# A fourth buffer for the cast and low part of the attention probabilities, in space that the tile of split q and k does not use

## The chip, the cores and the metric

The kernel runs on one core of a Trainium2 chip. The metric is the device time of one execution in microseconds (us). The engines are named as in the profile: PE (TensorE: matmuls; PEld is its weight load), DVE (VectorE), ACT (ScalarE), POOL (GpSimd) and SP (SyncE, which issues nearly all DMAs here). Each engine works through its own instructions in a fixed order; an instruction that waits for a semaphore holds up all that stand behind it on the same engine.

## The reference

One layer of a transformer with two kinds of attention heads, on 2048 positions of width 1024, in float32:

```
u   = rms_norm(x, norm1_w);  p = u @ w_in          # 3072 columns: q, k, v of both kinds
# differential heads (4): two softmax maps a head
logits = q.k * scale + t5_bias, masked by chunks of 64
attn   = softmax(map 0) - lam * softmax(map 1);  y = attn @ v
# stick-breaking heads (8)
z      = q.k * scale
log_1mb = log_sigmoid(-z) for s < t, else 0
rem    = reverse_cumsum(log_1mb) - log_1mb
a      = exp(log_sigmoid(z) + rem) for s < t, else 0;  y = a @ v
# both: rms_norm of y a head, then
h = x + concat(y_diff, y_sb) @ w_out
out = h + (silu(u2 @ w_gate) * (u2 @ w_up)) @ w_down,   u2 = rms_norm(h, norm2_w)
```

## The kernel before

PE multiplies in float16. To keep float32's accuracy every operand is split in two: `hi`, the value cast to float16, and `lo`, the cast of what is left. A product is then three matmuls, hi*hi, hi*lo and lo*hi.

**Head groups.** `block` takes the heads in eight groups, `g` 0 to 3 for one differential head each and 4 to 7 for two stick-breaking heads each. For a group, `proj` computes 384 columns of `p` (q, k and v) for 16 tiles of 128 positions: a tile of normed, transposed `x` is read back from DRAM as `xt` (line 395, three buffers), and 24 matmuls (line 329) go to `pj`. `proj_out` splits v into `v`, and q and k into `st` (lines 348 to 354). Each four tiles `proj_batch` transposes `st` by DMA into `qT` and `kT` (line 381). In the differential groups it first norms q and k, with `st` also as scratch for their squares (line 363). The projection of the next group is issued in between the attention of the present one (`advance`).

**Units of attention.** A unit is a block of 128 queries against up to 1024 keys. The differential `probs` makes z by scores, maximum, `Exp` and the subtraction of the two maps (line 516). The stick-breaking `stage_a` has for every 512 keys: scores on PE (`sc`), two sigmoids on ACT (lines 563, 566), a running product on DVE (line 568) and a product on DVE or POOL (line 569). Either way the probabilities of a unit then go through `split_t`:

```
s16 = s16p.tile([P, 2048], F16, tag="s16", bufs=SB, name=nm("s16"))
to16(s16[:, :n], src, n, he)
tt(s16[:, n : 2 * n], src, s16[:, :n], ALU.subtract, n, le)
aT = sp.tile([P, 16, P], F16, tag="aT", bufs=AB, name=nm("aT"))
SP.dma_start_transpose(aT[:, : 2 * n // P, :], s16[:, : 2 * n])
```

The cast (line 89 on ACT, line 93 on POOL) and the low part (line 98, on POOL) fill one `s16`, SP issues one transposing DMA from it into `aT` (line 412), and `pv` multiplies `aT` by v on PE (line 467). In the profile `s16` is called `s`. A buffer of `s16` is free again when its transpose has landed. There are `SB` = 3 of them and `AB` = 5 of `aT`; the stick-breaking part runs `pv` of a unit `PD` = 5 units after its `stage_a`.

**Output projection and feed-forward.** During the last group `out_proj` multiplies the finished rows by `w_out` and adds `x`, which it loads into `xf`, a tile with the tag of `st` (line 763) or spare space. `post` norms the rows and makes the seven combinations of blocks for the feed-forward part; they are split in tiles with the tag of `s16` as well (line 797, `x` in the profile) and stored to `xcd`. The feed-forward part follows, with its own pools over the space of the attention's pools.

**What sets the order.** The tile framework orders each engine's instructions when the program is built, with priorities and a simulated timeline (line 1238), and allots the buffers as it goes: an instruction that fills a tile has to come after the last use of that buffer's earlier tile. Which engine makes a cast or a subtraction is decided earlier, by the running cost sums of `pick` (lines 76 to 98), which do not know of buffers.

**Space.** The pool `s16p` (`bias` and the `s16` tiles) is on the left side of SBUF with `sp` and `zp`; `pp`, which holds `st`, is on the right side.

Of the kernel before, what the change touches and what calls it, by code (L numbers as in the profile page):

```python
# [11 lines left out]
F32 = mybir.dt.float32  # L12
F16 = mybir.dt.float16
# [8 lines left out]
S, D, P = 2048, 1024, 128  # L22
# [13 lines left out]
KW = {"A": 1.0, "D": 1.0, "P": 1.0}  # L36
AHEAD = 2
AHN = 0
QB, KB, ZB, AB, SB, PD = 4, 7, 9, 5, 3, 5
XL = (0, 4, 5, 2, 1, 6, 3)  # L40
CU = 3
WE = "AP"
# [17 lines left out]
def block(tc, a, out):  # L60
# [3 lines left out]
    with top:  # L64
# [8 lines left out]
        def note(e, ns):  # L73
            load[e] += ns * KW[e]
# [34 lines left out]
        def nm(s):  # L109
            uid[0] += 1  # L110
            return f"{s}{uid[0]}"
# [146 lines left out]
        pp = pjs.enter_context(tc.tile_pool(name="pp", bufs=2, side="right"))  # L258

        with ExitStack() as ph1:  # L260
# [61 lines left out]
            @pri("pm")  # L322
            def proj_tile(G, xt):
                pj = psj.tile([P, 512], F32, tag="pj", name=nm("pj"))
                xv = xt[:].rearrange("p (s k n) -> p s k n", s=2, k=KT)
                n = 0
                for kt in range(KT):
                    for xi, wi in ((0, 0), (0, 1), (1, 0)):
                        PE.matmul(pj[:, :384], lhsT=xv[:, xi, kt, :], rhs=G["w"][:, wi, kt, :], start=n == 0, stop=n == 23)  # L329
                        n += 1  # L330
                return pj
# [10 lines left out]
            @pri("po")  # L342
            def proj_out(g, G, pj, B, j):
                st, v, raw = B
                nv = 1 if g < 4 else 2
                vv = v[:, j, :].rearrange("p (h s e) -> p h s e", h=nv, s=2)
                split_psum(vv[:, :, 0, :], vv[:, :, 1, :], pj[:, 256:384].rearrange("p (h e) -> p h e", h=nv), 128)
                if g < 4:
                    if pick(A=270, D=335) == "A":
                        ACT.mul(raw[:, j, :], pj[:, :256], 2.0 ** -11)  # L350
                    else:
                        DVE.tensor_scalar(raw[:, j, :], pj[:, :256], 2.0 ** -11, None, op0=ALU.mult)
                else:
                    split_psum(st[:, 0:4, j, 0, :], st[:, 0:4, j, 1, :], pj[:, :256].rearrange("p (c e) -> p c e", c=4), 256)
# [33 lines left out]
            def proj(g, G, fresh=None):  # L388
                for t in range(NT):
                    if fresh is not None:  # L390
                        feed(t)
                        xt = ahead.pop(0)
                    else:
                        xt = pp.tile([P, 2 * D], F16, tag="xt", bufs=3, name=nm("xt"))
                        SP.dma_start(xt[:], xs[t])
                    if t % 4 == 0:
                        st = pp.tile([P, 6, 4, 2, 64], F16, tag="st", name=nm("st"))
                        v = sp.tile([P, 4, 256], F16, tag="v", bufs=KB, name=nm("v"))
                        raw = pp.tile([P, 4, 256], F32, tag="raw", name=nm("raw")) if g < 4 else None
                    pj = proj_tile(G, xt)  # L400
                    proj_out(g, G, pj, (st, v, raw), t % 4)
                    if t % 4 == 3:
                        proj_batch(g, G, (st, v, raw))
                    yield
# [223 lines left out]
            def feed(t):  # L628
                while nx[0] < min(NT, t + AHEAD + AHN):
                    nq.append(fresh(nx[0]))  # L630
                    nx[0] += 1
                while nx[1] < min(NT, t + AHEAD):
                    ahead.append(fresh_t(*nq.pop(0)))
                    nx[1] += 1
# [68 lines left out]
            def proj_stream():  # L703
                for g in range(NG):
                    for t, _ in enumerate(proj(g, Gs[g], fresh if g == 0 else None)):
                        if g == 0 and t == 0:
                            build_bias()
                        if g == NG - 1 and t in WT:
                            if t == WT[0]:
                                rp2.extend(norm_gain(a["norm2_w"], w2))  # L710
                            load_wo(WT.index(t))
                        if t == PF and g + 1 < NG:
                            Gs[g + 1] = load_w(g + 1)
                        yield
# [40 lines left out]
            def out_proj():  # L755
                for t in range(NT):
                    mt = pp.tile([P, 2 * D], F16, tag="xt", bufs=3, name=nm("mt"))[:].rearrange("p (k n) -> p k n", k=KT)
                    with tc.high_priority(PRI["wm"]) if PRI["wm"] else nullcontext():
                        mts.append(SP.dma_start(mt, ms[t]))
                    if t in spare:  # L760
                        xf = spare[t].bitcast(F32)
                    else:
                        xf = pp.tile([P, 6, 4, 2, 64], F16, tag="st", name=nm("xf"))[:].rearrange("p c t s e -> p (c t s e)").bitcast(F32)[:, :D]
                    SP.dma_start(xf, x[t * P : (t + 1) * P, :])
                    for h in range(2):
                        po = psj.tile([P, 512], F32, tag="pj", name=nm("po"))
                        for n in range(2):
                            q = 0
                            sl = slice(256 * n, 256 * n + 256)
                            for kt in range(KT):  # L770
                                for xi, wi in ((0, 0), (0, 1), (1, 0)):
                                    PE.matmul(po[:, sl], lhsT=mt[:, kt, P * xi : P * xi + P], rhs=wos[2 * h + n][wi][:, kt, :], start=q == 0, stop=q == 23)  # L772
                                    q += 1
                            xl = xf[:, 512 * h + 256 * n : 512 * h + 256 * n + 256]
                            DVE.scalar_tensor_tensor(xl, po[:, sl], kos[2 * h + n][:], xl, op0=ALU.mult, op1=ALU.add)  # L775
                    note("D", 1400)
                    SP.dma_start(hd[t], xf)
                    if t >= 12:
                        yield
                        continue  # L780
                    post(t, xf)
                    yield
# [3 lines left out]
            @pri("ox")  # L786
            def post(t, xf):
                if t % 2 == 0:
                    held[:] = [z4(), z4()]
                xn = held[t % 2]  # L790
                norm_tile(xf, xn[:, :D], w2)
                for h in range(2):
                    ACT.copy(xn[:, 512 * h : 512 * h + 512], transposed(xn, 512 * h)[:])
                note("D", 1150)
                note("A", 1000)
                if t % 2 == 1:
                    for _ in x_ops([z[:, :D].rearrange("p (d n) -> p d n", d=2) for z in held], z4()[:, :D].rearrange("p (d n) -> p d n", d=2), t // 8, t % 8 // 2, lambda: s16p.tile([P, 2048], F16, tag="s16", bufs=SB, name=nm("x16"))[:]):
                        pass

            op = out_proj()  # L800
            outs = 0
            advance(NT - LAG0)
# [439 lines left out]
```

## Time and profile before

| | |
|---|---|
| median of 3 runs | 2723.46 us (2717.96 to 2725.68) |
| the profiled execution | 2726.11 us |
| its span, first to last instruction | 2724.3 us |
| mean granted TensorE clock | 0.975 |

A wait in the profile is written `engine tile line <- what ended it: us in total, times, longest`. In a row of a table of stretches, each engine has its busy us and its count of instructions; after them stand the granted clock, the busy share of the 16 DMA engines and GB/s. A share over 1 is possible, since packets overlap in an engine. SP only issues, and has no busy time in these tables.

### The profile page before, as it was taken

The page shows a single profiled execution, that of the slowest core. Times are in us where ns is not written, and L with a number is a line of the kernel's source. Part 1 is how long each engine was busy: PE and PEld are TensorE (multiplying, and loading weights), DVE is VectorE, ACT ScalarE, POOL GpSimd, SP SyncE. Part 2 cuts the span into 40 slices and gives each one's busy share as a digit, 9 for nine tenths or more (in the row PEclk, how much of TensorE's full clock was granted, in tenths as well). Part 3 has the DMA queues.
Part 4 walks back from the last instruction along what each step waited for, and adds up shares of the span by engine and source line. Part 5 has one row for each costly group of instructions (what it writes and reads, how often), then busy time and mean ns, then how long its engine had stood idle before and what let it go on. Part 6 is the DMA issues. An engine that isn't in the chain of part 4 may idle for free. (4 is left out here: it accounts for less than half of the span.)

```text
span 2724.3 us, 45559 instructions
## 1 busy us (share of the span) xinstructions
PE 2471.4 (91%) x17084; PEld 1404.6 (52%) x17084; DVE 1945.7 (71%) x3716; ACT 1345.8 (49%) x2483; POOL 1569.3 (58%) x1134
## 2 busy tenths in 40 slices
PE   7998989898888786779888999999999999999998
PEld 4655655555555453557775444444444444444443
DVE  6898979698888988876666877777786544444445
ACT  4665656567878878765644535444352112111121
POOL 2577767667767777765655666575674232323223
PEclk9999999999999997999999999999999999999999
DMA  6788797779999998996797675666749744545534
GB/s 223 205 168 176 149 195 161 177 170 206 208 207 203 205 183 159 205 202 199 203 268 266 237 245 201 220 215 212 251 170 350 279 175 145 224 151 190 208 125 166
DMA packets 649134, 551.92 MB, mean 203 GB/s; under 512 B 506624, under 2 KB 574208, under 8 KB 638672
## 3 DMA queue, kind: packets, MB, share of 16 engines
q1 hardware_dynamic: 647088, 546.92, 73.2%
q8 instruction: 134, 2.20, 0.3%
q0 software_dynamic: 512, 1.36, 0.2%
q10 hardware_dynamic: 1312, 0.72, 0.1%
q14 instruction: 88, 0.72, 0.1%
HBM read 265.27 MB, written 151.52 MB: 153 GB/s over the span
## 5 line engine op out<-in xcount | busy, mean ns | idle before, releaser
L329 PE MATMUL pj<-w,xt 128*128 128x384 f16 x3072 | 570.1, 333 | 26.3 <-DVE st L339 10.8
L98 POOL TENSOR_TENSOR s<-z,s 128x1024 f16<-128x1024 f32 (+7 forms) x288 | 477.5, 1667 | 99.3 <-ACT s L89 94.8
L329 PEld LDWEIGHTS <-xt 128*128 128x128 f16 x3072 | 298.5, 100 | 233.8 <-issue 38.2
L568 DVE TENSOR_TENSOR_SCAN z<-z,sc 128x512 f32<-128x512 f32 (+3 forms) x320 | 352.9, 1112 | 81.4 <-ACT sc L566 39.3
L1048 PE MATMUL pd<-wd,act 128*128 128x512 f16 x1848 | 405.3, 379 | 3.9 <-DVE hs L1054 2.4
L457 PE MATMUL sc<-kT,qT 128*128 128x512 f16 (+3 forms) x1280 | 339.6, 357 | 51.7 <-DVE z L568 16.2
L467 PE MATMUL yp<-v,aT 128*128 128x64 f16 (+1 forms) x4896 | 279.6, 207 | 91.5 <-DMA aT<-s 90.4
L467 PEld LDWEIGHTS <-aT 128*128 128x128 f16 x4896 | 242.2, 101 | 181.9 <-DMA aT<-s 120.2
L98 POOL TENSOR_TENSOR act<-cg,act 128x512 f16<-128x512 f32 x117 | 166.3, 1434 | 239.4 <-ACT act L1006 133.1
L950 PEld LDWEIGHTS <-wg 128*128 128x128 f16 x1848 | 181.1, 98 | 222.0 <-issue 7.9
L1048 PEld LDWEIGHTS <-act 128*128 128x128 f16 x1848 | 180.6, 98 | 222.7 <-issue 4.8
L950 PEld LDWEIGHTS <-wu 128*128 128x128 f16 x1848 | 181.9, 99 | 219.0 <-issue 6.5
L98 POOL TENSOR_TENSOR hs<-hs,cu 128x512 f32<-128x512 f32 x132 | 166.9, 1269 | 220.9 <-DVE hs L1054 76.0
L98 POOL TENSOR_TENSOR fst<-fst 128x512 f32<-128x512 f32 x97 | 182.6, 1883 | 161.3 <-DVE wd L224 89.9
L1054 DVE SCALAR_TENSOR_TENSOR hs<-pd,c,hs 128x512 f32<-128x512 f32 x192 | 141.6, 748 | 155.6 <-PE pd L1048 151.9
L89 ACT CAST s<-z 128x384 f16<-128x384 f32 (+7 forms) x216 | 171.6, 800 | 133.5 <-DMA aT<-s 104.5
L563 ACT ACTIVATE z<-sc,c 128x512 f32<-128x512 f32 (+3 forms) x320 | 207.0, 650 | 25.7 <-PE sc L457 18.5
L569 POOL TENSOR_TENSOR z<-z,z 128x512 f32<-128x512 f32 (+3 forms) x148 | 151.5, 1027 | 100.7 <-DVE z L568 85.6
L772 PE MATMUL po<-wo,mt 128*128 128x256 f16 x1536 | 180.1, 276 | 20.2 <-DVE xf L775 11.2
L1006 ACT CAST act<-cg 128x512 f16<-128x512 f32 x132 | 81.1, 616 | 218.1 <-DVE cg L1012 173.6
L950 PE MATMUL pm<-X,wg 128*128 128x512 f16 x792 | 179.7, 380 | 0.0
L950 PE MATMUL pm<-X,wu 128*128 128x512 f16 x792 | 179.4, 379 | 0.0
(237 smaller groups left out, 4139.3 us busy)
## 6 DMA issues: line engine op xcount, KB each, us to landing
xt<-xs SPq DMA_DIRECT2D x112, 512.0 KB, 4.2
hs<-hd SPq DMA_DIRECT2D x96, 512.0 KB, 4.4
hd<-hs SPq DMA_DIRECT2D x80, 512.0 KB, 4.4
split<-wg SPq DMA_DIRECT2D x11, 1792.0 KB, 11.3
split<-wu SPq DMA_DIRECT2D x11, 1792.0 KB, 10.4
split<-wd SPq DMA_DIRECT2D x11, 1792.0 KB, 10.5
wg<-split SPq DMA_DIRECT2D x11, 1792.0 KB, 7.2
wd<-split SPq DMA_DIRECT2D x11, 1792.0 KB, 8.9
```

Of the source, the lines that this page charges most:

```text
L89: ACT.copy(dst, src)
L98: (DVE if e == "D" else POOL).tensor_tensor(dst, a_, b_, op)
L329: PE.matmul(pj[:, :384], lhsT=xv[:, xi, kt, :], rhs=G["w"][:, wi, kt, :], start=n == 0, stop=n == 23)
L457: PE.matmul(sc[:, : 128 * w].rearrange("p (t n) -> p t n", n=P), lhsT=G["q"][i // 4][:, 2 - 2 * o + m, i % 4, :], rhs=G["k"][q][:, m, 0:w, ...
L467: PE.matmul(yp[:, y0 : y0 + wd], lhsT=aT[:, a_, :], rhs=v[:, v_ : v_ + wd], start=start and j == 0 and q == 0, stop=stop and j == nb - 1 a ...
L563: ACT.activation(om[:, lo:hi], sc[:, :w], AF.Sigmoid, scale=G["nkz"][:])
L568: DVE.tensor_tensor_scan(ov, ov, sc[:, :w], om[:, hi : hi + 1], op0=ALU.mult, op1=ALU.bypass)
L569: (DVE if e == "D" else POOL).tensor_tensor(be[:, lo:hi], beta, om[:, lo + 1 : hi + 1], ALU.mult)
L772: PE.matmul(po[:, sl], lhsT=mt[:, kt, P * xi : P * xi + P], rhs=wos[2 * h + n][wi][:, kt, :], start=q == 0, stop=q == 23)
L950: PE.matmul(ps_[:].rearrange("p (t n) -> p t n", n=P), lhsT=wv[:, wo, wi, 128 * kt : 128 * kt + 128], rhs=X[xo][:, :, xi, kt, :], start=st ...
L1048: PE.matmul(po[:], lhsT=act[:, ao, xi, 128 * j : 128 * j + 128], rhs=W["d"][:, wo, wi, :], start=start and u == 0 and q == 0, stop=u == nu ...
L1054: DVE.scalar_tensor_tensor(dst, po[:], kd[:], src, op0=ALU.mult, op1=ALU.add)
```

## The change

The tile `st` has room for six chunks of 64 columns, of which four are used: two of q and two of k. The change makes it four chunks wide, here and where `out_proj` takes a tile of the same tag for `xf`. `SB` goes from 3 to 4.

```
-QB, KB, ZB, AB, SB, PD = 4, 7, 9, 5, 3, 5
+QB, KB, ZB, AB, SB, PD = 4, 7, 9, 5, 4, 5
...
-                        st = pp.tile([P, 6, 4, 2, 64], F16, tag="st", name=nm("st"))
+                        st = pp.tile([P, 4, 4, 2, 64], F16, tag="st", name=nm("st"))
...
-                        xf = pp.tile([P, 6, 4, 2, 64], F16, tag="st", name=nm("xf"))[:].rearrange("p c t s e -> p (c t s e)").bitcast(F32)[:, :D]
+                        xf = pp.tile([P, 4, 4, 2, 64], F16, tag="st", name=nm("xf"))[:].rearrange("p c t s e -> p (c t s e)").bitcast(F32)[:, :D]
```

## The prediction

> **What bounds the kernel now.** I read the busy shares and the 40 slices first, then tables of stretches, the waits of one stretch, and last a piece of the timeline.
>
> ```profile
> span 2724.3 us, 45559 instructions
> PE 2471.4 (91%) x17084; PEld 1404.6 (52%) x17084; DVE 1945.7 (71%) x3716; ACT 1345.8 (49%) x2483; POOL 1569.3 (58%) x1134
> PE   7998989898888786779888999999999999999998
> L467 PE MATMUL yp<-v,aT 128*128 128x64 f16 (+1 forms) x4896 | 279.6, 207 | 91.5 <-DMA aT<-s 90.4
> L89 ACT CAST s<-z 128x384 f16<-128x384 f32 (+7 forms) x216 | 171.6, 800 | 133.5 <-DMA aT<-s 104.5
> ```
>
> PE carries the program, and its only large wait is 90.4 us for `aT`, the transposed probabilities. ScalarE's casts into `s16`, the tile of which there will be four, sit idle 104.5 us until a transpose out of an older `s16` has landed. The next rows say where the span has room: us of the stretch, then busy us (and instruction counts) of PE, PEld, DVE, ACT, POOL, then clock, DMA share and GB/s.
>
> ```profile
> 115.00:250.00 135.00, 122.44 (x980) 78.52 (x978) 123.76 (x382) 83.96 (x217) 95.02 (x69) 0.99 0.78 164
> 115.00:630.00 515.00, 461.42 (x3694) 296.65 (x3693) 438.57 (x1314) 313.55 (x803) 359.96 (x257) 0.98 0.80 170
> 630.00:1125.00 495.00, 405.56 (x4271) 257.33 (x4268) 415.94 (x759) 392.52 (x722) 367.80 (x273) 0.94 1.01 198
> 700.00:800.00 100.00, 85.47 (x920) 54.32 (x918) 85.28 (x158) 78.07 (x137) 75.53 (x51) 0.98 1.13 215
> 1125.00:1400.00 275.00, 230.71 (x2420) 183.32 (x2419) 195.56 (x314) 167.76 (x296) 179.09 (x128) 0.96 0.83 201
> 1400.00:1450.00 50.00, 44.57 (x403) 39.24 (x401) 28.58 (x50) 17.12 (x19) 23.74 (x17) 1.00 1.00 374
> 1450.00:2724.00 1274.00, 1237.03 (x5789) 569.83 (x5786) 784.19 (x1091) 396.81 (x522) 592.22 (x407) 0.99 0.58 209
> ```
>
> From 1450 us on (the feed-forward part, with no `s16`) PE is busy 97% and nothing is to be had. The differential heads, 115 to 630, hold PE at 90%. The stick-breaking heads of groups 4 to 6, 630 to 1125, are where no engine is full: DVE 84%, PE 82%, ACT 79%, POOL 74%. The waits of that stretch (total, times, longest):
>
> ```profile
> ACT s L89 <- DMA aT<-s: 67.5, 50, 3.6
> PE yp L467 <- DMA aT<-s: 42.1, 38, 3.7
> POOL s L98 <- ACT s L89: 60.4, 49, 5.0
> DVE z L568 <- ACT sc L566: 31.8, 32, 2.3
> DVE z L568 <- ACT z L566: 30.2, 23, 3.9
> PE pj L329 <- DMA xt<-xs: 4.2, 4, 1.4
> ```
>
> ACT is idle 495 - 392.5 = 102.5 us there, and 67.5 of it is casts that wait for a free `s16`. ACT issues in order, so the sigmoids of the next units stand behind such a cast. That is what DVE (62.0 us for ACT's sigmoids), POOL (60.4 us for the cast) and, at the end, PE (42.1 us for `aT`) wait for. One case, and the size of one lap of a buffer in that stretch:
>
> ```profile
> 869.77 11.62 SPq L412 DMA_TRANSPOSE aT<-s  x4
> 878.46 0.51 ACT L89 CAST s<-z 128x384 f16<-128x384 f32 x1 [2.33 <-DMA aT<-s]
> ```
>
> ```profile
> L89 ACT CAST s<-z x146: 297/938/1172, 631.7 to 1124.8; 128x1024 f16<-128x1024 f32 x60, 128x128 f16<-128x128 f32 x13, 128x256 f16<-128x256 f32 x13, 128x384 f16<-128x384 f32 x12
> L98 POOL TENSOR_TENSOR s<-z,s x146: 425/1887/3647, 629.5 to 1123.3; 128x1024 f16<-128x1024 f32 x61, 128x128 f16<-128x128 f32 x13, 128x256 f16<-128x256 f32 x12, 128x384 f16<-128x384 f32 x12
> L412 SPq DMA_TRANSPOSE aT<-s x147: 1167/1775/6477, 631.7 to 1124.7; - x147
> DMA to landing us min/median/max: 2.3/4.5/9.1
> ```
>
> By the medians a buffer is held for cast 0.94, low part 1.89 and transpose 4.5, 7.3 us, plus the waits between. One unit comes every 495/147 = 3.37 us, so three buffers allow a lap of 10.1 us, and waits of 2.8 us use that up; four allow 13.5 us.
>
> **The change part by part.** *The space.* `st` shrinks from 6 to 4 chunks of 4 x 2 x 64 f16, 6144 to 4096 bytes a partition, in two buffers: 4096 bytes freed. A fourth `s16` of 2048 f16 takes 4096. No line reads chunks 4 and 5: lines 354, 363, 379 and 381 stay in the first four, and line 763 uses 1024 f32, exactly 4096 bytes. No instruction, DMA or byte moved is added; engine choices by `pick` see no buffer counts. So the only direct effect is that a cast waits for the landing four units back instead of three, which is one unit (3.37 us) earlier on average; no cast wait of the stretch is longer than 3.6 us. I count the stalls of 67.5 us as gone. The low part and the transpose wait for nothing new: `aT` keeps five buffers.
>
> *What it is worth from 630 to 1125.* Below by nothing: the work freed may only queue at the next resource. Above by the tightest of four: the stall itself, 67.5; DVE filled as in its fullest row here, 123.76/135 = 0.917, which would need 415.94/0.917 = 454 us, so 41; PE as in the differential stretch, 461.42/515 = 0.896, 405.56/0.896 = 453, so 42; the DMA engines at the share of 700 to 800, 495 x 1.01/1.13 = 442, so 53. Between 0 and 41 I look at the row nearest to the floor, the DMA busy share of this stretch in its own 40 slices:
>
> ```profile
> DMA  7999999999999979998999999995999998668989
> xt<-xs SPq DMA_DIRECT2D x46, 512.0 KB, 4.4
> ```
>
> Nearly every slice of 12.4 us is at 90% or more, so landings will lengthen when transposes are asked for sooner, and part of the stall comes back as landing time. I take 0.4 of 41, 16 us.
>
> [...]
>
> *The other stretches with `s16`.* The first three rows below are of 115 to 630, the last three of 1125 to 1400.
>
> ```profile
> ACT s L89 <- DMA aT<-s: 19.1, 6, 5.3
> POOL s L93 <- DMA aT<-s: 3.5, 4, 1.5
> PE yp L467 <- DMA aT<-s: 28.9, 19, 4.1
> ACT s L89 <- DMA aT<-s: 18.3, 10, 6.0
> ACT s L89 <- DMA xcd<-x: 12.0, 6, 4.8
> PE yp L467 <- DMA aT<-s: 19.4, 15, 3.2
> ```
>
> In the differential stretch the buffer stalls are 22.6 us on engines that are 61% (ACT) and 70% (POOL) busy, so most of it is slack: bounds 0 and 22.6, I take 3. In the last group the ring is shared with `post`'s `x16` tiles (12.0 us); ACT is 61% busy; bounds 0 and PE's 19.4, I take 3.
>
> *The feed-forward pools.* They are laid over the space of `sp`, `zp` and `s16p`, which now ends 4096 bytes higher, so one of their tiles may wait for another old tile. PE is idle 5.4 us in all from 1400 to 1450, where those pools fill for the first time; such waits cannot save more than that, and I bound their cost by the same. I take 0, the middle.
>
> *The order.* The program is ordered by the tile framework's planner with a simulated timeline (line 1238), which allots buffers while it orders. With a fourth buffer it may order ACT, POOL and SP differently up to 1400 us. No row prices that; its ends are rivals 2 and 3, and I take 0.
>
> Sum: 16 + 3 + 3 = 22 us. The profiled execution took 2726.1 us, 1.8 more than its span: 2726.1 - 22 = 2704. The median of the runs is 2723.5, 2.6 lower, so 2701.5; I say **2702 us**.
>
> **The rivals.** *1, the DMA engines are the wall: no change.* The cast no longer waits, but the transposes wait in SP's queue or in the DMA engines. For it: the slices of 9, and transposes that take 6.5 us to issue at most against 1.2 at least. Against it: 700 to 800 ran at 1.13, and PE was at 85% there, above the stretch's 82%. Gain 0 to 8 us, 2716 to 2724, say 2720. [...]
>
> *2, everything freed is used.* The planner's order and the chip both follow the wider ring, and the upper bounds come true: 41 in the middle, half of 22.6 and of 19.4 beside it, 62: 2723.5 - 62 = 2662, say 2668. Against it: the DMA row.
>
> *3, slower: the projection's loads come late.* SP issues in order. In the middle stretch 46 loads of `xt` and 147 transposes share it. If ready transposes now stand ahead of the loads, each load behind one more is issued 1.8 us later and lands behind 4.5 us of transpose traffic. With three buffers of `xt`, PE loses only 4.2 us to them now. From the point where a third of the 46 (15) come late by 1.8 + half of 4.5, 4 us, PE loses 60 us, against the 22 won: 2723.5 + 38 = 2761; with half of that lateness hidden by prefetch, 2723.5 + 8 = 2732. I take 2735. For it: SP's transposes can hold it up to 6.5 us each. Against: the loads have little wait today, and the prefetch covers three tiles of 24 matmuls.
>
> *4, the ring is not what the chip waits for.* The release comes from the `aT` side, so the same waits stand: 2723. Against: all 50 waits name the landing of the transpose out of `s`, which frees that buffer and no other.
>
> **How the numbers follow.** A difference of about 0.3% (8 us) is what a measurement of this kernel tells from none; the three runs spread over 7.7 us. Chances: forecast 0.45 (own range 2690 to 2714), rival 1 0.17, rival 2 0.13, rival 3 0.21, rival 4 0.04. Faster: 0.45 + 0.13 = 0.58; same 0.17 + 0.04 = 0.21; slower 0.21. The range takes the upper bound of the gains (2668) and rival 3 up to 2736; beyond it lie the worst of rival 3 and the rest of rival 2, 2 in 10.
>
> **What would show it.** In the stretch that runs groups 4 to 6: ACT's 67.5 us of `s` <- `aT` under 20; the stretch itself shorter by about 16; PE's wait for `aT` in the whole program down from 90.4 to some 65; DMA share above 1.01 and the median landing above 4.5. If the landing grows to 6 or more with PE's wait unchanged, rival 1 holds. If PE waits over 25 us for `xt`, rival 3. The feed-forward stretch should keep its 1274 us within 3. I am wrong if the cast's wait goes and the stretch keeps its length, or if its order on ACT has changed so far that other waits take the place.

## The result, and the profile after

The changed kernel is slower. Its median is 2733.35 us (2730.81 to 2738.48, 7 runs), that of the kernel before beside it 2725.61 us (2717.96 to 2727.47, 7 runs): ratio 1.0036, 95% interval 1.0024 to 1.0048. The ratios here and below compare all runs of the two kernels, not only their medians. I had forecast 2702 us and a faster kernel. The profiled execution took 2732.98 us. Three executions of 2947, 3369 and 10660 us, two of the kernel before and one of the first turned pair below (whose only profile is of it, and is not read), are left out of all numbers.

The page of the changed kernel, busy shares and then the groups of which the prediction spoke (busy us, mean ns | idle us before them, and the cause of most of it):

```profile
span 2731.2 us, 45588 instructions
PE 2472.4 (91%) x17084; PEld 1408.6 (52%) x17084; DVE 1948.5 (71%) x3716; ACT 1344.8 (49%) x2483; POOL 1567.7 (57%) x1134
L467 PE MATMUL yp<-v,aT 128*128 128x64 f16 (+1 forms) x4896 | 281.4, 208 | 102.2 <-DMA aT<-s 101.7
L569 POOL TENSOR_TENSOR z<-z,z 128x512 f32<-128x512 f32 (+3 forms) x148 | 151.7, 1029 | 140.8 <-DVE z L568 104.8
L89 ACT CAST s<-z 128x384 f16<-128x384 f32 (+7 forms) x216 | 170.4, 801 | 106.1 <-POOL z L569 37.3
```

PE is busy for as long as before (2471.4 to 2472.4 us), so 5.9 of the 6.9 us of longer span are time in which PE stands still. ScalarE's casts no longer wait mainly for a free `s16`; their first cause is now POOL's line 569, 37.3 us. The buffer did at that place what it was made for. But PE's wait for `aT` is longer (90.4 to 101.7 us), and POOL's line 569 waits 104.8 us for DVE's scan at line 568 (85.6 before).

The waits of 630 to 1125 us (us, times, longest), and the stretches of 115 to 630, 630 to 1125 and 1450 to 2724 (columns as in the prediction):

```profile
PE yp L467 <- DMA aT<-s: 54.0, 44, 3.4
POOL s L98 <- ACT s L89: 45.7, 32, 4.6
ACT s L89 <- DMA aT<-s: 27.7, 21, 4.6
DVE z L568 <- ACT sc L566: 26.9, 27, 3.5
DVE z L568 <- ACT z L566: 9.9, 14, 3.2
PE pj L329 <- DMA xt<-xs: 3.4, 3, 2.2
```

```profile
115.00:630.00 515.00, 457.66 (x3652) 294.44 (x3651) 428.89 (x1291) 308.54 (x790) 353.44 (x251) 0.97 0.79 166
630.00:1125.00 495.00, 402.20 (x4206) 256.75 (x4204) 416.87 (x760) 388.55 (x713) 364.25 (x271) 0.93 0.98 197
1450.00:2724.00 1274.00, 1245.82 (x5896) 578.98 (x5893) 782.61 (x1092) 397.91 (x524) 596.86 (x408) 0.99 0.58 210
```

The cast's stall fell from 67.5 to 27.7 us, DVE's waits for the sigmoids from 62.0 to 36.8, POOL's for the cast from 60.4 to 45.7. Yet fewer matmuls fit into each of the first two stretches (4206 for 4271, 3652 for 3694), and work that was done by 1450 before stands behind it now (5896 for 5789). To see where the time went I counted the 288 transposes into `aT` in the order of their issue and took the landing of the 96th (end of the differential heads), of the 240th and of the last, us from the start of the span:

| | 96th | 240th | 288th | span |
|---|---|---|---|---|
| before | 636.1 | 1124.8 | 1394.5 | 2724.3 |
| changed | 646.2 | 1135.1 | 1404.6 | 2731.2 |

In these two profiles all of the loss, 10.1 us, is there by the 96th. The stick-breaking groups take 488.9 us where they took 488.7, and the part behind the last landing takes 3.2 us less. The differential heads, for which I had priced the change at -3 us, are where these two profiles part. The size is uncertain, since one profile stands for each kernel. Two versions below that have the kernel before's order up to there (the narrow `st` alone, and the fourth tile in the stick-breaking heads alone) land the 96th at 638.6 and 640.8 us; one with the changed kernel's order (the fourth tile in the differential heads alone) lands it at 642.4. The second half of the differential heads, 360 to 640 us, has no single new stall; DVE's waits, kernel before and then changed:

```profile
DVE z L492 <- PE sc L457: 10.2, 11, 2.0
DVE v L339 <- ACT v L336: 7.0, 4, 2.5
```

```profile
DVE z L492 <- PE sc L457: 18.5, 14, 5.2
DVE v L339 <- ACT v L336: 13.4, 8, 3.4
```

Together these two are 14.7 us longer, in short waits with no buffer in them: an instruction stands at the head of DVE's list (the order in which the engine issues) before its scores or its `v` are there. Other waits of DVE shrank, and its idle time in that stretch grew by 7.7 us in all (50.0 to 57.7). The lists themselves differ. The change adds no instruction, but it has the planner write a new list for each engine: 17325 lines of PE's (weight loads counted) stand differently, and 121 of ScalarE's 216 casts stand earlier. In the traces the two kernels issue alike up to some 160 us, and apart from there on.

### The profile page after: what moved, and what is told of

Same layout as the page of the kernel before. It is cut to its first block, busy times and chain, and to the rows that moved or that the text cites. A ratio compares the mean times of both kernels' runs of the same rounds, so it can differ in the third digit from the quotient of the medians.

```text
span 2731.2 us, 45588 instructions
## 1 busy us (share of the span) xinstructions
PE 2472.4 (91%) x17084; PEld 1408.6 (52%) x17084; DVE 1948.5 (71%) x3716; ACT 1344.8 (49%) x2483; POOL 1567.7 (57%) x1134
## 5 line engine op out<-in xcount | busy, mean ns | idle before, releaser
L98 POOL TENSOR_TENSOR s<-z,s 128x1024 f16<-128x1024 f32 (+7 forms) x288 | 477.4, 1670 | 61.3 <-ACT s L89 57.7
L457 PE MATMUL sc<-kT,qT 128*128 128x512 f16 (+3 forms) x1280 | 338.5, 359 | 54.8 <-DVE z L568 13.9
L467 PE MATMUL yp<-v,aT 128*128 128x64 f16 (+1 forms) x4896 | 281.4, 208 | 102.2 <-DMA aT<-s 101.7
L569 POOL TENSOR_TENSOR z<-z,z 128x512 f32<-128x512 f32 (+3 forms) x148 | 151.7, 1029 | 140.8 <-DVE z L568 104.8
L89 ACT CAST s<-z 128x384 f16<-128x384 f32 (+7 forms) x216 | 170.4, 801 | 106.1 <-POOL z L569 37.3
```

Source lines behind the costliest of these rows:

```text
L89: ACT.copy(dst, src)
L98: (DVE if e == "D" else POOL).tensor_tensor(dst, a_, b_, op)
L457: PE.matmul(sc[:, : 128 * w].rearrange("p (t n) -> p t n", n=P), lhsT=G["q"][i // 4][:, 2 - 2 * o + m, i % 4, :], rhs=G["k"][q][:, m, 0:w, ...
L467: PE.matmul(yp[:, y0 : y0 + wd], lhsT=aT[:, a_, :], rhs=v[:, v_ : v_ + wd], start=start and j == 0 and q == 0, stop=stop and j == nb - 1 a ...
L569: (DVE if e == "D" else POOL).tensor_tensor(be[:, lo:hi], beta, om[:, lo + 1 : hi + 1], ALU.mult)
```

## The experiments

All ratios are against the kernel before, run on the same chip in the same series (its median was 2725.6 to 2728.0 us), with 95% intervals.

**The space, the buffer and the list, one at a time.** The first kernel has the narrow `st` and three buffers; its lists are those of the kernel before.

```
-QB, KB, ZB, AB, SB, PD = 4, 7, 9, 5, 4, 5
+QB, KB, ZB, AB, SB, PD = 4, 7, 9, 5, 3, 5
```

> The narrower st alone, with three buffers of s16. Every engine's instructions stand in the order of the kernel before. Theory O (the time came with the planner's new order): within 0.3% of the kernel before, ratio 1.000. Theory R (the fourth buffer costs time on the chip by itself, through the DMA engines or POOL): the same, 1.000. Theory S (the moved addresses and the pools laid over them cost it): slower by about 0.3%, ratio 1.003 or more.

Measured: 2727.63 us, 1.0004 (0.9991 to 1.0017). Space and addresses cost nothing that can be told from noise.

The second is the whole change, with every engine held to the list of the kernel before. The program is laid out twice: the first pass, with `SB = 3`, only yields the order, which the second, with `SB = 4`, has to keep.

```
+PINNED = ("PE", "Activation", "DVE", "Pool", "SP")
...
+        if i.engine in last:
+            tc.add_manual_dep(i, last[i.engine], ..., reason="issue order")
+        last[i.engine] = name
...
+    kept, SB = SB, 3
+    plan = build()
+    SB = kept
+    nc = build([i.name for f in plan.m.functions for bb in f.blocks for i in bb.instructions])
```

> The whole change, four buffers, but each engine issues its instructions in exactly the order of the kernel before: the program is planned twice, first with three buffers, and the second plan is tied to the order of the first. Theory O: the loss of 0.36% is gone and the buffer shows what it is worth by itself; if the forecast's chain is right (casts set free, then sigmoids, scans, transposes), 16 to 22 us faster than before, ratio 0.992 to 0.994, with the casts' wait for a transpose near zero in 630 to 1125. If the ring only takes the blame for a wait that something else sets, the casts' wait falls and the ratio stays at 0.998 to 1.001. Theory R: ratio 1.003 or more although the order is the old one.

Measured: 2714.11 us, 0.9956 (0.9940 to 0.9972). On the old list the buffer is worth 12 us; against that, the new list costs 0.80%, 22 us. This version beats both kernels, and its trace has the sequence of the kernel before on every engine. The gain lies between the two ranges that were expected (0.992 to 0.994 if the forecast's chain was right, 0.998 to 1.001 if the ring only took the blame), and the casts' wait did not come near zero. Two of its waits from 630 to 1125 us:

```profile
PE yp L467 <- DMA aT<-s: 52.5, 43, 3.1
ACT s L89 <- DMA aT<-s: 28.3, 18, 3.3
```

And two groups of its page:

```profile
L467 PE MATMUL yp<-v,aT 128*128 128x64 f16 (+1 forms) x4896 | 280.1, 207 | 97.5 <-DMA aT<-s 97.0
L89 ACT CAST s<-z 128x384 f16<-128x384 f32 (+7 forms) x216 | 172.9, 804 | 77.1 <-DMA aT<-s 31.4
```

The cast's stall in that stretch is 28.3 us here and 27.7 in the changed kernel, PE's wait for `aT` 52.5 and 54.0, and the two kernels lie 0.8% apart. The waits at the ring do not tell a good list from a bad one.

**Half of the program each.** Of four successive units, the fourth takes a tile of its own (`s4`), in units 97 to 288 only (stick-breaking heads) or in units 1 to 96 only (differential heads).

```
+                units16[0] += 1
+                s16 = s16p.tile([P, 2048], F16, tag="s4", bufs=1, ...) if FOURTH[0] <= units16[0] <= FOURTH[1] and units16[0] % 4 == 0 else s16p.tile([P, 2048], F16, tag="s16", bufs=SB, ...)
```

> The fourth buffer only for units of the stick-breaking groups (every fourth of them goes to it); the differential groups keep three, and their order is that of the kernel before. By unit counts the changed kernel lost about 10 us before 640 us and little after. Theory O, with the loss in the differential part: that part as before, so the whole 5 to 10 us below the changed kernel, ratio to before 0.998 to 1.001. If the stick-breaking part's new order costs as much by itself: 1.003 again.

> The opposite: the fourth buffer only for the differential groups; their order is that of the changed kernel. Theory O, with the loss in the differential part: group 3's last unit lands about 10 us late again, and the ratio is 1.002 to 1.005. If the differential part's lateness is made up later in any order: 1.000.

Measured: 2722.94 us, 0.9986 (0.9972 to 1.0000), with the fourth tile in the stick-breaking heads; 2742.99 us, 1.0058 (1.0038 to 1.0078), with it in the differential heads. So the version with the old list in the differential heads is the faster one, by 0.7%; the second was dearer than expected (1.002 to 1.005). But each of the two also has a list of its own in the stick-breaking heads, and the traces do not put the loss in one place: the second lands its 96th at 642.4 us and its 240th at 1142.3, 6.3 and 17.5 us later than the kernel before, so that 11.2 us are lost in the stick-breaking heads, where it has three buffers (its profiled execution, 2735.55 us, is the fastest of its six). That the differential heads' list is the dear part is not shown.

**Is it one engine's list?** The whole change, with one engine alone held to the old list and the others listed anew around it.

```
+PINNED = ("Activation",)      # e5
+PINNED = ("PE",)              # e6
```

> The whole change, four buffers; ScalarE alone issues its 2483 instructions in the order of the kernel before, the planner lists the other engines around that. The kernel with four buffers and every engine in the old order stood at 0.9956, the changed kernel at 1.0036. Theory T (the loss has one place: the casts that the new order puts earlier on ScalarE, 121 of 216, stand ahead of work that is needed sooner): most of the loss goes with ScalarE's order, ratio 0.994 to 0.999, and the sum of the waits of VectorE's L568 for ScalarE between 630 and 1125 us stays below 55 us. Theory C (no one place: the order before is one that happens to run well, and any list that departs from it in thousands of places loses some 0.3 to 1%): PE's order still departs in about 11000 lines, so the ratio is 1.000 to 1.006.

> The whole change, four buffers; TensorE alone keeps the order of the kernel before, the planner lists the other four engines around that. Theory P (what the new order spoils is TensorE's own list: a matmul that waits for a transposed aT or for ScalarE's result stands ahead of others that are ready; TensorE's waits for aT between 115 and 1125 us rose from 71.0 to 86.5 us): ratio 0.994 to 0.999. Theory T (the loss is in ScalarE's list) and theory C (any departure costs): the ratio stays at 1.000 to 1.006.

Measured: 1.0064 (1.0044 to 1.0084), 2746.49 us, with ScalarE in the old order; 1.0015 (1.0003 to 1.0027), 2732.81 us, with TensorE. Theory T falls: with the early casts gone from ScalarE's list the kernel is no faster, although the waits at line 568 that it named are 43.1 us, below its 55. Theory P falls too, though less far. Theory C's range holds the second figure; the first is just above it. Neither ScalarE's list nor TensorE's holds the loss by itself. The test is a blunt one, since holding one list has the planner write the others anew, and VectorE, GpSimd and SyncE were not held alone.

**New lists with no fourth buffer.** The kernel before, with one pair of VectorE instructions told to stand in the other order. That alone has the planner write everything behind it anew.

```
+        for first, then in SWAP:
+            tc.add_manual_dep(traced[then], first, ..., reason="issue order")
```

> The kernel before, three buffers, nothing of the change; two instructions of VectorE in the first 400 us are told to stand in the other order, and the planner lists everything behind them anew: 17396 lines of TensorE's list stand differently, about as many as in the changed kernel (17325). Theory C (any list that departs so far from the order before loses): ratio 1.003 to 1.010 without any fourth buffer. Theory T or P (the loss belongs to what the fourth buffer does to the list): ratio 0.998 to 1.002.

> As the run before this one with another pair: the kernel before with three buffers, two instructions of VectorE late in the differential heads told to stand in the other order; TensorE's list departs from there on, in 11703 lines. Theory C: ratio 1.002 to 1.008, and a different figure from the other pair's, since the lists are different ones. Theory T or P: 0.998 to 1.002.

Measured: 1.0042 (1.0026 to 1.0057) and 1.0037 (1.0024 to 1.0051); medians 2739.45 and 2739.29 us. So two lists that depart from the old one cost as much as the whole change did, without the change. Theory C holds.

**The same lists with four buffers.** The lists of those two runs, on every engine, in a kernel with `SB = 4`.

> The list of the run e10_swap_dve2 (made for three buffers, 1.0037 with three) on every engine, but the tile has four buffers. Theory A (two separate things add up: a fourth buffer is worth some 0.5% on a given list, and each list has a price of its own): 1.0037 - 0.0048 = 0.999, 0.997 to 1.001. Theory U (the fourth buffer pays only on the list of the kernel before): 1.002 to 1.006.

> The list of the run e8_swap_dve (made for three buffers, 1.0042 with three) on every engine, with four buffers. Theory A: 1.0042 - 0.0048 = 0.9994, 0.997 to 1.0015. Theory U: 1.002 to 1.007.

Measured: 0.9964 (0.9952 to 0.9976), 2718.29 us, and 0.9995 (0.9984 to 1.0006), 2725.99 us. Theory U falls. The first is better than theory A's range, the second inside it.

**The other way round: the changed kernel's list with three buffers.** Some casts on ScalarE's list rely on a fourth buffer, so ScalarE is listed anew.

```
-    kept, SB = SB, 3
+    kept, SB = SB, 4
...
+PINNED = ("PE", "DVE", "Pool", "SP")
```

> Three buffers, but TensorE, VectorE, GpSimd and SyncE issue in the order of the changed kernel; ScalarE is listed anew around them, since some of its casts stand where only a fourth buffer can be free (717 lines of its list depart from the changed kernel's). Theory A: 1.0036 + 0.0048 = 1.008, 1.005 to 1.014. Theory U: the fourth buffer is worth nothing on this list, 1.001 to 1.006.

Measured: 2774.88 us, 1.0169 (1.0154 to 1.0183), more than theory A said. A list made for four may lean on the fourth; ScalarE's new list is in the figure too, so that this is not shown apart. Its page shows the stall back where it was:

```profile
L89 ACT CAST s<-z 128x384 f16<-128x384 f32 (+7 forms) x216 | 170.4, 797 | 151.2 <-DMA aT<-s 102.4
```

**Are lists made for four buffers worse as such?** Three more of them, each the changed kernel with one pair of VectorE instructions turned round; a third three-buffer list run with four; and a list made for two, run with four.

> The changed kernel, four buffers, with the two VectorE instructions of e10_swap_dve2 told to stand in the other order: up to there the list of the changed kernel, behind it another list made for four buffers (12705 lines of TensorE's differ from the changed kernel's). Theory A with prices of lists that scatter: a figure of its own between 0.997 and 1.009, away from 1.0036 by more than 0.0015 in either direction. A theory by which four buffers make the planner's lists worse as such: 1.002 to 1.006 again.

> Four buffers, a list made for four: the changed kernel with two VectorE instructions of the first 300 us told to stand in the other order, so that nearly all behind them is listed anew (1999 places of TensorE's list where the next instruction is another one; the changed kernel has 1967 against before's). Theory M: 1.001 to 1.008, like the changed kernel. Theory K: anywhere from 0.994 to 1.008, and with the next run at least one of the two below 1.000.

> As the run before with a pair further on in the differential heads (1556 such places against the changed kernel's list). Theory M: 1.001 to 1.008. Theory K: anywhere from 0.994 to 1.008.

> Four buffers, every engine in a list made for three buffers: that of the kernel before with two VectorE instructions of the stick-breaking heads told to stand in the other order (TensorE's list departs in 11734 lines from before's). Theory M (margin: a list made for fewer buffers than there are leaves a buffer in hand for what the planner times wrongly, a list made for all of them doesn't): 0.994 to 1.000. Theory K (chance: lists scatter by some 0.3% whatever they were made for): anywhere from 0.994 to 1.008, as the lists made for four.

> Four buffers, every engine in the list that the planner makes for two buffers (21064 lines of TensorE's depart from before's). Theory M in its simple form: two buffers in hand, 0.992 to 0.999. Against it: with two buffers the planner has to hold units back that the chip could start, so the list itself may be poorer, 1.000 to 1.010. Theory K: anywhere from 0.994 to 1.010.

Measured: 1.0017 (1.0007 to 1.0028), 0.9967 (0.9953 to 0.9980) and 0.9977 (0.9966 to 0.9987) for the lists made for four; 1.0006 (0.9993 to 1.0018) for the one made for three; 1.0206 (1.0185 to 1.0228), 2786.34 us, for the one made for two. Theory M falls: two lists made for four are faster than the kernel before, one made for three is not, and the list with two buffers in hand is the slowest of all. Theory K, that lists scatter whatever they were made for, stands for the first four of these; the list made for two lies outside every range expected of it (at most 1.010). The second of the lists made for four took 2719.27 us, and its page begins:

```profile
span 2717.3 us, 45598 instructions
```

It has the change word for word but for one turned pair, and its span is 13.9 us shorter. Its 96th, 240th and last landings are at 647.2, 1120.0 and 1384.7 us: as late as the changed kernel in the differential heads, and 16 us quicker through the stick-breaking heads. So a late 96th landing does not by itself make a slow kernel.

**Is the list of the kernel before an ordinary one?** Two more lists with three buffers and nothing of the change.

> The list of the run e16_swap3_four (1.0006 with four buffers), with the three that it was made for; nothing of the change is in it. Theory A (the fourth buffer is worth 0.4 to 0.7% on a given list): 1.0006 + 0.0055 = 1.006, 1.004 to 1.009. If the kernel before's list is not a favourable one, some three-buffer list should come out below 1.000, and this is the fourth.

> The kernel before, three buffers, with a fourth pair of VectorE instructions (stick-breaking heads) told to stand in the other order; 11164 lines of TensorE's list depart. If the list of the kernel before is a favourable one among those the planner could make: 1.002 to 1.006, as the other two; if it is an ordinary one: as likely below 1.000 as above.

Measured: 1.0045 (1.0029 to 1.0061), 2738.73 us, and 1.0025 (1.0013 to 1.0036), 2734.66 us. Of five three-buffer lists that of the kernel before is the fastest; the other four stand at 1.0025 to 1.0045, mean 1.0037.

**The sum of it.** The buffer's worth on a fixed list:

| list | three buffers | four buffers | difference |
|---|---|---|---|
| of the kernel before | 1.0004 | 0.9956 | -0.0048 |
| first pair turned | 1.0042 | 0.9995 | -0.0047 |
| second pair turned | 1.0037 | 0.9964 | -0.0073 |
| third pair turned | 1.0045 | 1.0006 | -0.0039 |

Each difference is good to about 0.002. The mean is -0.0052, 14 us of 2726. The 10 us of 1.0036 can then be put as -14 for the buffer, +10 for leaving the kernel before's list (the mean of 1.0037), and +14 for a list drawn worse than the mean; the last term is what is left over, not measured. The four lists made for four buffers have a mean of 0.9999, 10 us below the one that was drawn, and spread over 0.7%. What makes one list 13 us better than another is not put down to one instruction, and stays open.

The pages show that list and buffer do not reach the time in one way. PE makes the same 17084 matmuls in every version; from each page its span, its busy time, the rest as idle time, and the clock:

| kernel | span | PE busy | PE idle | granted clock |
|---|---|---|---|---|
| before | 2724.3 | 2471.4 | 252.9 | 0.975 |
| before, narrow `st` | 2727.9 | 2469.7 | 258.2 | 0.973 |
| changed | 2731.2 | 2472.4 | 258.8 | 0.971 |
| list of before, four buffers | 2715.6 | 2470.4 | 245.2 | 0.975 |
| second pair, three buffers | 2736.8 | 2483.8 | 253.0 | 0.968 |
| second pair, four | 2715.7 | 2462.2 | 253.5 | 0.973 |
| third pair, three | 2739.0 | 2485.8 | 253.2 | 0.967 |
| third pair, four | 2724.8 | 2471.2 | 253.6 | 0.973 |
| fourth pair, three | 2735.7 | 2483.7 | 252.0 | 0.970 |

The first two rows, two kernels with one list, show how far single profiles scatter: 5 us of idle time, 2 us of busy time; the changed kernel's 5.9 us more of idle time are hardly clear of that. On the list of the kernel before the buffer shortens PE's idle time. On the second and third turned lists PE stands still as long as before, and both the list's price and the buffer's gain lie in the time for which PE is busy, at a lower clock with three buffers than with four. The rows for the second pair, three buffers and then four:

```profile
PE 2483.8 (91%) x17084; PEld 1412.8 (52%) x17084; DVE 1953.9 (71%) x3716; ACT 1345.3 (49%) x2483; POOL 1570.3 (57%) x1134
PE 2462.2 (91%) x17084; PEld 1399.7 (52%) x17084; DVE 1952.7 (72%) x3716; ACT 1344.4 (50%) x2483; POOL 1570.9 (58%) x1134
```

No run holds the clock while the list changes, so whether a new list costs time by its waits or by way of the clock stays open as well.

## Why the prediction was wrong

- **What bounds the kernel.** Right that PE carries the program and that the casts' stall names a real release: with three buffers on the changed kernel's list (ScalarE's listed anew) it is 102.4 us over the program, with four 27.7 us there and 31.4 on the old list.
- **"I count the stalls of 67.5 us as gone."** Mis-sized: 27.7 us remained in the stretch (28.3 on the old list). A lap of four was to allow 13.5 us against some 7.3 and waits of 2.8; instead the ring filled further and the units waited elsewhere in it. Followed unit by unit through the traces, a buffer is held for 9.0 us in that stretch with three, 10.2 in the changed kernel and 9.9 on the old list. The time from the transpose's issue to its landing is 4.6, 4.5 and 4.6; what grew are the pauses between cast, low part and issue, from 2.0 to 3.3 and 2.9 us. The test "under 20" failed.
- **16 us from 630 to 1125.** Too large. On the old list the 96th to the 240th landing take 483.8 us (633.9 to 1117.7) against 488.7, a gain of 4.9, near the lower bound and within rival 1's 0 to 8; on the second and third turned lists the fourth buffer brings 12.2 and 6.0 us there (498.7 to 486.5, 497.3 to 491.3). That other list, the second made for four, took 472.8 us, after a late start: the list decides more than the buffer.
- **3 and 3 for the differential heads and the last group.** On the old list 2.2 and 1.6 us (633.9 for 636.1; 268.1 for 269.7 from the 240th landing to the last). That is no more than the narrow `st` alone moves the same stages, with the same list (2.5 us later, 4.2 less). On the second and third turned lists the buffer brings 8.5 us by the 96th landing (637.3 to 628.8 on both), so there the 3 for the differential heads was too small. The whole sum of 22 us measured 12 on the old list and 11 to 20 on the other three.
- **"No row prices that; its ends are rivals 2 and 3, and I take 0."** The step that failed. The new list costs 22 us over the old one with the same four buffers, more than the buffer brings. Rivals 2 and 3 were not its ends either: I had thought of the order as something that decides where the buffer's gain goes, in the stretch with the ring's stall. It is a separate draw for the whole program up to 1400 us, PE's list included, of which the prediction did not speak. Against the old list with four buffers the changed kernel is 12.3 us later at the 96th landing and 18.8 at the last, by one profile each.
- **Rival 3** had the sign and nearly the time (2735), by another cause. PE's wait for `xt` at line 329 is 3.4 us in the stretch, and 25 were to show it. The loads did not come late.
- **Rival 1**'s test, landings of 6 us or more, is not met (median 4.4 us over the program, before and after), and the list that passes the same stretch in 16 us less speaks against a wall there. The DMA share did not rise above 1.01 as I had said (0.98; 1.00 on the old list). Rival 2's 41 us came on no list. Rival 4 falls: the buffer moves the time on all four lists.
- **Feed-forward pools at nothing.** Right within a few us: from the last landing to the end 1326.6 us, before 1329.8.
- **The tests.** The stretch of the stick-breaking groups was to be 16 us shorter and kept its length (488.9 us). PE's `aT` wait was to fall to 65 and rose to 101.7, but it also rose to 97.0 in the version that is 12 us faster. It was no test of the gain. The last sentence of the prediction, that other waits could take the stall's place if the order on ACT changed, is what happened, though not on ACT alone.

The repeating gap that named the buffer stood on ACT, 104.5 us before its casts, not on PE. The runs show that a buffer was short, worth 0.4 to 0.7% on each of four lists. They show it for a list that stays as it is, and this change did not leave it so.

## What to carry to other kernels

Where a planner orders the program, a change in a buffer count is two changes: the buffer, and a new list for every engine, which here scatters by some 0.2 to 0.4% either way. Price the list as a draw, and remember that a tuned kernel's list may be a lucky one that any edit gives up: here 0.37% on average, against 0.52% for the buffer. To measure the buffer, hold the old list; to use it, try several lists or keep the old one with the new buffer, which here gave 0.9956.

## What the runs showed of the hardware

The mean granted clock goes with the list. Over all timed runs the mean is 0.974 for the kernel before (102 runs, 0.968 to 0.980) and 0.974 and 0.976 for the two kernels with its list (12 and 7 runs); for every other list it is lower, from 0.961 (the list made for two, 1.0206) to 0.972 (the second turned pair with four buffers, 0.9964), and 0.969 for the changed kernel. Within the runs of one kernel a clock lower by 0.001 goes with about 0.9 us of span, loosely. I can't tell cause from effect: in the changed kernel the clock is 0.93 from 630 to 1125 us, where PE is busy 81%, and 0.99 in the feed-forward stretch, where it is busy 98%, and no run shows which of the two brings the other. For the changed kernel it is no explanation by itself, since PE's busy time grew by only 1.0 us. For the three turned lists with three buffers in the table above it may be: their spans are 11 to 15 us longer than that of the kernel before, their PE busy times 12 to 14 us, at clocks of 0.967 to 0.970 against 0.975.
